# A two-layer hybrid trunk on one core: where the first mean stands, the order of attention's maxima, one late remainder, and how means are read

## The chip, the core and the metric

The kernel runs on one core of a Trainium2 chip. A core has TensorE (matmuls; in the profile PE, and PEld for its weight loads), VectorE (DVE), ScalarE (ACT), GpSimd (POOL) and SyncE (SP), which run side by side and wait for each other by semaphores, and 16 DMA engines that move data between the chip's main memory and the on-chip memory. TensorE writes its results to eight banks of 512 float32 columns by 128 rows; DVE and ACT read them from there. The metric is the time of one execution in device microseconds (us), as the median of several runs.

## The reference

Two layers, on 512 tokens of width 1024, all float32. The reference, cut to what matters:

```python
for l in range(DEPTH):                                             # 2 layers
    x = x + 0.5 * swiglu(rms_norm(x, ffn1_norm[l]), ffn1_w_in[l], ffn1_w_out[l])   # 1024 -> 2 x 2816 -> 1024
    h = rms_norm(x, mix_norm[l]) @ w_mix_in[l]                     # one projection for three mixers
    (c_x, c_b, c_c, h_q, h_f, h_i, h_g, f_q, f_k, f_v, f_f) = jnp.split(h, split_at, axis=-1)
    y = jnp.concatenate([
        short_conv_mixer(c_x, c_b, c_c, conv_w[l]),                # gated causal convolution, 3 taps, 256 channels
        hgrn2_mixer(h_q, h_f, h_i, h_g, ...),                      # 4 heads, linear recurrence, output norm per head
        fox_mixer(f_q, f_k, f_v, f_f, ...),                        # 8 heads, causal softmax attention with decay
    ], axis=-1)
    x = x + y @ w_mix_out[l]
    x = x + 0.5 * swiglu(rms_norm(x, ffn2_norm[l]), ffn2_w_in[l], ffn2_w_out[l])
```

`rms_norm` divides by the root of a mean of squares, `swiglu` is `(silu(gate) * up) @ w_out`. The attention subtracts each row's maximum before the exponential, as a softmax does.

## The kernel before

**Numbers.** Every large product is made of three matmuls (`mm3`, lines 494, 500 and 501): an operand is split into a high part, rounded by ACT (a cast, L475 or L1017), and a low part, the remainder, which DVE subtracts (L481 or L1019); high times high, high times low and low times high are added up in one bank. Activations are held with features on the rows and tokens on the columns. The moving operand of these matmuls is read `woven`: token t of the first half, token t of the second half, token t+1 of the first, and so on; the bank then holds the two halves alternating, and who reads it takes it apart again (`unwoven`).

**Feed-forward.** The hidden width has 22 tiles of 128. The first few (`covered`: 6 in the first feed-forward, 4 in the others) are made from the raw `x` in units of two tiles, eight steps along the depth in pairs, while the norm of `x` is still being made; `clear` divides the result by the norm afterwards. What else is done in that time stands in the table `ENTRY` by a due number: number n is the n-th pair of steps, and `deal(n)` is called ahead of each pair. It was also called at one quarter and at three quarters of a pair, for the due numbers of the means that end in .25 or .75. At a mean's due number `squares` has TensorE sum the squares of all features (`sum_norm`, L701 and L702, a matrix of 1/1024 times high and low part of the squares); at the due number of "norm" `take_norm` makes the inverse root out of it with a logarithm, two exponentials or squares on ACT and a Newton step on DVE. In the first feed-forward the mean has 4.25 and the norm 5; the second unit of two tiles starts at 4. There DVE first copies the mean out of the bank (L714).

The remaining tiles are worked in three chunks by a scheme that multiplies 2x2 blocks with seven products P1 to P7; `plan` lays the steps into the hidden layer ("I") and out of it ("O") in one sequence. Weights are cast three steps ahead (`LEAD`). The order of the work of ACT, DVE, SP and POOL in this part is written out (`follow`), as is TensorE's. In the last feed-forward a step out of the hidden layer adds its results into `xT` from the banks (L1090) in its second half (g = 1). A pair of hidden tiles of the last chunk leaves a split still to be made, a cast (L1228) and a subtraction (L1229); it is kept in `late` and made in the step after.

**Mix.** The mixers share TensorE: the generator `dense` (projections of attention), the convolution's projections and the output projection run beside `fox_attend`; the tuple `BESIDE` says how many pieces of them go between two steps of attention. Each head has two parts: p = 0 has the first two blocks of 128 queries in one bank, p = 1 the other two in a bank each. A part is: a mask into the bank and four matmuls (L1917); a maximum per block on DVE (L1933); an exponential on ACT with the row sums (L382, called at `scores`); the division; transposes (L1953), split into high and low (L1968, L1969); the products with the values (L1978). The output of a head is summed from two halves of the bank by DVE (L1996, two instructions), after ACT has copied one half (L1992). Here only TensorE's order is written out; that of DVE and ACT is chosen by the framework's planner from the order of the program, priorities and its own estimates of times. `add_manual_dep` with NOSYNC fixes an order of two instructions on an engine without a semaphore. Banks are guarded as a whole: an instruction of one engine on a bank waits for that of another engine ahead of it in the program.

The convolution's result is multiplied by its gate in `conv_out` (L1518), cast (L1520) and split (L1521), for its first tile and then its second (i = 1).

The HGRN mixer takes a mean over each head's 64 features with two matmuls (L1751, L1752) and the same `rsqrt`.

Of the kernel before, what the change touches and what calls it, by code (L numbers as in the profile page):

```python
# [14 lines left out]
ALU = mybir.AluOpType  # L15
# [235 lines left out]
class Trunk:  # L251
# [257 lines left out]
    def stream_steps(  # L509
# [17 lines left out]
        while k < nk:  # L527
# [60 lines left out]
            for n, ((acc, cols, toks, *more), j) in enumerate(order):  # L588
# [4 lines left out]
                for part in (1, 3) if deal is not None else ():  # L593
                    if n == part * len(order) // 4:
                        deal(k, part / 4)
# [76 lines left out]
    def rsqrt(self, out, v, r, t):  # L672

        nc = self.nc
        return [
            ("a", self.act(t, r, AF.Square)),
            ("v", nc.vector.scalar_tensor_tensor(
                out=t, in0=v, scalar=EPS, in1=t, op0=ALU.add, op1=ALU.mult
            )),
            ("v", nc.vector.tensor_scalar(t, t, scalar1=-0.5, scalar2=1.5, op0=ALU.mult, op1=ALU.add)),  # L680
            ("v", nc.vector.tensor_mul(out, r, t)),
        ]
# [14 lines left out]
    def sum_norm(self, bank, pool):  # L697
        if self.sqparts is None:
            self.part_norm(pool)
        (hi, lo), self.sqparts = self.sqparts, None  # L700
        self.nc.tensor.matmul(bank, self.ones_mean, hi, start=True, stop=False)  # L701
        return self.nc.tensor.matmul(bank, self.ones_mean, lo, start=False, stop=True)  # L702

    def take_norm(self, bank, pool, copied=False):

        mean = bank
        r = pool.tile([P, T], F32, tag=self.tt, name=self.n("nr"), bufs=self.tb)
        t = pool.tile([P, T], F32, tag=self.tt, name=self.n("nt"), bufs=self.tb)
        self.table(LNEXP)
        i = [("a", self.act(r, bank, AF.Ln, bias=self.epsc)), ("a", self.act(r, r, AF.Exp, scale=-0.5))]  # L710
        self.inv = self.res.tile([P, T], F32, tag="inv", name=self.n("inv"))
        if copied:
            mean = self.sqacc
            i.append(("v", self.nc.vector.tensor_copy(mean, bank)))  # L714
        return i + self.rsqrt(self.inv, mean, r, t)
# [228 lines left out]
    def halved(self, fp, w_in, w_out, covered, deal):  # L944
# [194 lines left out]
        for n, (kind, w, p) in enumerate(seq):  # L1139
# [87 lines left out]
            for hh, hl, y in late:  # L1227
                A(nc.scalar.copy(hh, y))  # L1228
                V(nc.vector.tensor_sub(hl, y, hh))  # L1229
            late = inner  # L1230
# [283 lines left out]
    def conv_out(self, pool, i, pb):  # L1514
# [3 lines left out]
        nc.vector.tensor_mul(halves(u), unwoven(pb), halves(y))  # L1518
# [5 lines left out]
    def hgrn(self, l, pr, hp, z, q, v, sg, og, S, kb, b, both):  # L1524
# [93 lines left out]
        halves = lambda lev: lambda a, i: a.rearrange(  # L1618
# [3 lines left out]
        def operands(lev):  # L1622
            w, half = 2**lev // 2, halves(lev)
# [20 lines left out]
        def score(lev, e, sb, at):  # L1644
# [9 lines left out]
            for i in range(4):  # L1654
                for hh, par in ((0, 0), (1, 1), (0, 1), (1, 0)):
# [4 lines left out]
                        out.rearrange("p (n w) -> p n w", w=2**lev // 2), keys, halves(lev)(keys, 1),  # L1660
# [3 lines left out]
        def place(lev, sb, at):  # L1664

            w, half = 2**lev // 2, halves(lev)
# [84 lines left out]
        nc.tensor.matmul(mb, self.ones_blk, sqh, start=True, stop=False)  # L1751
        nc.tensor.matmul(mb, self.ones_blk, sql, start=False, stop=True)  # L1752
        r, t = tmp(), tmp()
        self.act(r, mb, AF.Ln, bias=self.epsc)
        self.act(r, r, AF.Exp, scale=-0.5)
        self.rsqrt(r, mb, r, t)
# [138 lines left out]
    def fox_attend(self, pool, half, g):  # L1895
# [11 lines left out]
        def scores(h, p):  # L1907
# [22 lines left out]
            to = [pb[:, :P], pb[:, P:]] if p == 0 else [pb[:, : 3 * P], pb[:, 3 * P :]]  # L1930
            for u in range(2):
                o = slice(u, u + 1)
                nc.vector.tensor_reduce(nm[:, o], at[u], axis=AX.X, op=ALU.max, negate=True)  # L1933
                self.act(
                    turned_out(to[u]), inner(at[u]), AF.Exp,
                    bias=nm[:, o], accum_out=rs[:, o],
                )
# [33 lines left out]
        def values(h, p):  # L1971
# [22 lines left out]
            def add(to):  # L1994
                for n, b in ((0, slice(0, 4, 3)), (2, slice(1, 3))):
                    nc.vector.tensor_add(  # L1996
                        turned_out(to)[:, n : n + 2], inner(self.ob[:64, :])[:, b],
                        turned_out(ft[r, :])[:, b],
                    )

# [120 lines left out]
def trunk_kernel(  # L2121
# [5 lines left out]
    for l in range(DEPTH):  # L2127
        k.ffn(
            ffn1_w_in[l], ffn1_w_out[l], mix_norm[l], 4 if l else 6, 2 if l else 4.25,
# [39 lines left out]
```

## Time and profile before

| | |
|---|---|
| Median of 3 runs | 1742.44 us (1741.82 to 1742.48) |
| The profiled execution's own time | 1741.56 us |
| Its span, first to last instruction | 1739.8 us |
| TensorE: matmuls, weight loads | busy 1733.8 us (100%), 1627.5 us (94%) |
| DVE, ACT, POOL | busy 1413.9 us (81%), 1011.1 us (58%), 175.9 us (10%) |
| Granted TensorE clock | 1.000 of full speed |
| DMA | 262.29 MB, mean 151 GB/s |

A row of the timeline reads: start in us from the span's start, duration, engine, line of the program, operation, written tile <- read tiles, sizes, how many instructions are merged in the row, and in brackets the idle time of the engine just before, with what ended it. A row of the waits reads: engine, tile and line that waited <- engine, tile and line it waited for: us in total, times, longest. A row of the groups ends in busy us, mean ns of one instruction, and idle us before them. Matmuls are pipelined: the durations of neighbours overlap, so what a matmul costs is the distance of its start from the next one's.

### The profile page before, as it was taken

What the parts mean: (1) busy time and instruction counts of PE and PEld (TensorE: products, weight loads), DVE (VectorE), ACT (ScalarE), POOL (GpSimd) and SP (SyncE); (2) the same over time, 40 slices, a digit from 0 to 9 for tenths busy, and PEclk for the clock granted to TensorE, in tenths of its full rate; (3) what the DMA queues carried; (4) which work ended last, traced back from release to release, by engine and by line L of the source; (5) the groups of instructions that cost most, each with busy time, mean ns of one, the idle gap of its engine ahead of it and who ended that gap; (6) DMA issues with size and microseconds to landing.
All of it is one profiled execution on the core that took longest, in us unless ns stands there. A gap on an engine that the chain in (4) does not pass through costs nothing.

```text
span 1739.8 us, 32583 instructions
## 1 busy us (share of the span) xinstructions
PE 1733.8 (100%) x13215; PEld 1627.5 (94%) x13215; DVE 1413.9 (81%) x1926; ACT 1011.1 (58%) x1407; POOL 175.9 (10%) x174
## 2 busy tenths in 40 slices
PE   9999999999999999999999999999999999999999
PEld 7999999888888999999989999998888889999998
DVE  7988788778888898888689887876878779888884
ACT  5565565465766565566446556555657765655651
POOL 0011120100000112012001111201000000120210
PEclk9999999999999999999999999999999999999999
DMA  7768784243542966868267787923435437677672
GB/s 218 193 142 195 186 174 107 74 127 93 141 128 89 241 155 153 207 163 170 85 196 165 177 184 175 194 81 75 115 102 145 119 119 209 158 164 211 147 158 97
DMA packets 249766, 262.29 MB, mean 151 GB/s; under 512 B 25816, under 2 KB 221152, under 8 KB 249616
## 3 DMA queue, kind: packets, MB, share of 16 engines
q1 hardware_dynamic: 197344, 192.02, 37.0%
q0 software_dynamic: 52256, 68.19, 24.2%
q8 instruction: 104, 1.70, 0.4%
q14 instruction: 46, 0.38, 0.1%
q10 hardware_dynamic: 16, 0.00, 0.0%
HBM read 226.15 MB, written 2.17 MB: 131 GB/s over the span
## 4 chain that ended last, share of the span: by engine, by line
PE 96%; DVE 2%; ACT 1%; issue 0%; DMA 0%; SPq 0%; ACTq 0%
PE mm L494 10%; PE mm L501 10%; PE mm L500 10%; PE mm L580 9%; PE pt L500 7%; PE pt L494 7%; PE pt L501 7%; PE sc L500 6%; PE sc L494 6%; PE sc L501 6%; PE po L500 3%; PE po L494 3%; PE po L501 3%; PE po L580 2%; PE sc L1917 1%; PE po L1978 1%
## 5 line engine op out<-in xcount | busy, mean ns | idle before, releaser
L1019 DVE TENSOR_TENSOR hl<-w,hl 128x1024 fp32r<-128x1024 f32 x279 | 340.6, 1222 | 99.2 <-ACT hl L1017 97.9
L1017 ACT CAST hl<-w 128x1024 fp32r<-128x1024 f32 x279 | 292.6, 1049 | 204.3 <-PE mm L501 51.4
L481 DVE TENSOR_TENSOR hl<-st,hl 128x1024 fp32r<-128x1024 f32 (+3 forms) x152 | 159.8, 1054 | 93.5 <-ACT hl L475 92.8
L475 ACT CAST hl<-st 128x1024 fp32r<-128x1024 f32 (+3 forms) x151 | 137.3, 912 | 149.4 <-PE po L501 43.5
L501 PE MATMUL mm<-xc,hl 128*128 128x256 f32 x696 | 191.7, 275 | 0.0
L500 PE MATMUL mm<-xc,hl 128*128 128x256 f32 x696 | 191.7, 275 | 0.0
L494 PE MATMUL mm<-xc,hl 128*128 128x256 f32 x698 | 191.7, 275 | 0.0
L494 PE MATMUL pt<-xc,hl 128*128 128x256 f32 x546 | 150.2, 276 | 0.0
L500 PE MATMUL pt<-xc,hl 128*128 128x256 f32 x544 | 149.8, 275 | 0.0
L501 PE MATMUL pt<-xc,hl 128*128 128x256 f32 x544 | 149.7, 275 | 0.0
L494 PEld LDWEIGHTS mm<-xc,hl 128*128 128x128 f32 x698 | 134.0, 192 | 0.1
L501 PEld LDWEIGHTS mm<-xc,hl 128*128 128x128 f32 x696 | 133.7, 192 | 0.4 <-DVE hl L1019 0.4
L500 PEld LDWEIGHTS mm<-xc,hl 128*128 128x128 f32 x696 | 133.7, 192 | 0.0
L494 PE MATMUL sc<-xc,hl 128*128 128x256 f32 (+1 forms) x466 | 128.0, 275 | 0.0
L501 PE MATMUL sc<-xc,hl 128*128 128x256 f32 x464 | 127.8, 275 | 0.0
L500 PE MATMUL sc<-xc,hl 128*128 128x256 f32 x464 | 127.8, 275 | 0.0
L580 PE MATMUL mm<-hl,x 128*128 128x512 f32 x432 | 107.3, 384 | 0.0
L494 PEld LDWEIGHTS pt<-xc,hl 128*128 128x128 f32 x546 | 104.7, 192 | 0.3
L500 PEld LDWEIGHTS pt<-xc,hl 128*128 128x128 f32 x544 | 104.5, 192 | 0.3
L501 PEld LDWEIGHTS pt<-xc,hl 128*128 128x128 f32 x544 | 104.5, 192 | 0.0
L494 PE MATMUL mm<-x,hl 128*128 128x512 f32 x272 | 103.8, 381 | 0.0
L501 PE MATMUL mm<-x,hl 128*128 128x512 f32 x272 | 103.1, 380 | 0.2 <-DVE hl L481 0.2
(542 smaller groups left out, 5314.7 us busy)
## 6 DMA issues: line engine op xcount, KB each, us to landing
w<-in_ffn_w_in_dram SPq DMA_DIRECT2D x124, 512.0 KB
w<-in_ffn_w_out_dram POOLq DMA_DIRECT2D x50, 512.0 KB, 9.6
w<-in_ffn_w_out_dram SPq DMA_DIRECT2D x49, 512.0 KB
st<-in_ffn_w_out_dram SPq DMA_DIRECT2D x39, 512.0 KB
st<-in_w_mix_in_dram SPq DMA_DIRECT2D x72, 256.0 KB
st<-in_ffn_w_in_dram SPq DMA_DIRECT2D x71, 256.0 KB
w<-in_ffn_w_in_dram POOLq DMA_DIRECT2D x29, 512.0 KB, 10.1
w<-S POOLq DMA_DIRECT2D x29, 512.0 KB, 5.1
```

The costliest lines, as they stand in the source:

```text
L475: a = nc.scalar.copy(hi, src[:, c : c + w])
L481: b = nc.vector.tensor_sub(lo, src[:, c : c + w], hi)
L494: i = nc.tensor.matmul(acc[:, c], ah, bh[:, c.start // 2 : c.stop // 2, :], start=first and c.start == 0, stop=False, skip_group_check=True,)
L500: nc.tensor.matmul(acc, ah, bl, start=False, stop=False, skip_group_check=True)
L501: i = nc.tensor.matmul(acc, al, bh, start=False, stop=last, skip_group_check=True)
L580: self.follow("p", self.nc.tensor.matmul(acc, *((w, woven(x)) if toks is None else (x[:, toks], woven(w))), start=k == 0 and id(acc) not i ...
L1017: A(nc.scalar.copy(hi, src))
L1019: return lambda: V(nc.vector.tensor_sub(lo, src, hi))
L1917: mm = lambda *a, **k: E(nc.tensor.matmul(*a, skip_group_check=True, **k))
L1978: E(nc.tensor.matmul(self.ob[:, o * P : (o + len(at)) * P], half[2][:, j, h].rearrange("p a d -> p (a d)"), turned_in(part[:, at[0] : at[- ...
```

## The change

Five edits.

1. The mean of the first feed-forward has due number 4 instead of 4.25, so it is called ahead of the second unit's first pair of steps; the call of `deal` at one quarter of each pair is taken out.
2. The sums of squares are read `woven`, in the feed-forwards' norms and in the HGRN norm, and the mean's bank is read `unwoven` by the logarithm, the Newton step and the copy.
3. In attention's first part (p = 0) both maxima are issued ahead of both exponentials. The output sums of a head (L1996) may not be placed on DVE ahead of the maximum that was issued last.
4. Neither may the multiplication of the convolution's second tile (L1518 with i = 1).
5. In the last feed-forward, where the next step is the second half of a step out of the hidden layer, the pending split stays pending for that step too.

The function `halves` inside the HGRN mixer is called `sides` in the new text, so that the outer `halves` can be used; nothing else of it changes.

```diff
@@ stream_steps
-                for part in (1, 3) if deal is not None else ():
-                    if n == part * len(order) // 4:
-                        deal(k, part / 4)
+                if deal is not None and n == 3 * len(order) // 4:
+                    deal(k, 0.75)
@@ rsqrt
+        back = halves(t) if len(v.shape) != len(t.shape) else t
...
-                out=t, in0=v, scalar=EPS, in1=t, op0=ALU.add, op1=ALU.mult
+                out=back, in0=v, scalar=EPS, in1=back, op0=ALU.add, op1=ALU.mult
@@ sum_norm
-        self.nc.tensor.matmul(bank, self.ones_mean, hi, start=True, stop=False)
-        return self.nc.tensor.matmul(bank, self.ones_mean, lo, start=False, stop=True)
+        self.nc.tensor.matmul(bank, self.ones_mean, woven(hi), start=True, stop=False)
+        return self.nc.tensor.matmul(bank, self.ones_mean, woven(lo), start=False, stop=True)
@@ take_norm
-        mean = bank
+        mean = unwoven(bank)
...
-        i = [("a", self.act(r, bank, AF.Ln, bias=self.epsc)), ("a", self.act(r, r, AF.Exp, scale=-0.5))]
+        i = [
+            ("a", self.act(halves(r), unwoven(bank), AF.Ln, bias=self.epsc)),
+            ("a", self.act(r, r, AF.Exp, scale=-0.5)),
+        ]
...
-            i.append(("v", self.nc.vector.tensor_copy(mean, bank)))
+            i.append(("v", self.nc.vector.tensor_copy(halves(mean), unwoven(bank))))
@@ halved
-            for hh, hl, y in late:
-                A(nc.scalar.copy(hh, y))
-                V(nc.vector.tensor_sub(hl, y, hh))
-            late = inner
+            if last and n + 1 < len(seq) and seq[n + 1][0] == "O" and seq[n + 1][1][1]:
+
+                late = late + inner
+            else:
+                for hh, hl, y in late:
+                    A(nc.scalar.copy(hh, y))
+                    V(nc.vector.tensor_sub(hl, y, hh))
+                late = inner
@@ conv_out
-        nc.vector.tensor_mul(halves(u), unwoven(pb), halves(y))
+        m = nc.vector.tensor_mul(halves(u), unwoven(pb), halves(y))
+        if i:
+            self.tc.add_manual_dep(m.ins, self.maxima, NOSYNC, reason="given order")
@@ hgrn
-        nc.tensor.matmul(mb, self.ones_blk, sqh, start=True, stop=False)
-        nc.tensor.matmul(mb, self.ones_blk, sql, start=False, stop=True)
+        nc.tensor.matmul(mb, self.ones_blk, woven(sqh), start=True, stop=False)
+        nc.tensor.matmul(mb, self.ones_blk, woven(sql), start=False, stop=True)
...
-        self.act(r, mb, AF.Ln, bias=self.epsc)
+        self.act(halves(r), unwoven(mb), AF.Ln, bias=self.epsc)
...
-        self.rsqrt(r, mb, r, t)
+        self.rsqrt(r, unwoven(mb), r, t)
@@ fox_attend, scores
+            def maximum(u):
+                m = nc.vector.tensor_reduce(
+                    nm[:, u : u + 1], at[u], axis=AX.X, op=ALU.max, negate=True
+                )
+                self.maxima = m.ins.name
+
+            if p == 0:
+                maximum(0)
+                maximum(1)
             for u in range(2):
                 o = slice(u, u + 1)
-                nc.vector.tensor_reduce(nm[:, o], at[u], axis=AX.X, op=ALU.max, negate=True)
+                if p:
+                    maximum(u)
@@ fox_attend, values, add
-                    nc.vector.tensor_add(
+                    a = nc.vector.tensor_add(
                         turned_out(to)[:, n : n + 2], inner(self.ob[:64, :])[:, b],
                         turned_out(ft[r, :])[:, b],
                     )
+                    self.tc.add_manual_dep(a.ins, self.maxima, NOSYNC, reason="given order")
@@ trunk_kernel
-            ffn1_w_in[l], ffn1_w_out[l], mix_norm[l], 4 if l else 6, 2 if l else 4.25,
+            ffn1_w_in[l], ffn1_w_out[l], mix_norm[l], 4 if l else 6, 2 if l else 4,
```

More of the change, by code (lines that the diff above doesn't have):

```diff
@@ L1617, in hgrn @@
         A8 = A.rearrange("p h i t -> p (h i) t")
-        halves = lambda lev: lambda a, i: a.rearrange(
+        sides = lambda lev: lambda a, i: a.rearrange(
             "p (n two w) -> p n two w", two=2, w=2**lev // 2
@@ L1622, in operands @@
         def operands(lev):
-            w, half = 2**lev // 2, halves(lev)
+            w, half = 2**lev // 2, sides(lev)
             e = tmp()
@@ L1659, in score @@
                     nc.tensor.matmul(
-                        out.rearrange("p (n w) -> p n w", w=2**lev // 2), keys, halves(lev)(keys, 1),
+                        out.rearrange("p (n w) -> p n w", w=2**lev // 2), keys, sides(lev)(keys, 1),
                         start=True, stop=True,
@@ L1664, in place @@
         def place(lev, sb, at):
-            w, half = 2**lev // 2, halves(lev)
+            w, half = 2**lev // 2, sides(lev)
             if lev < 2:
```

## The prediction

> **What bounds the kernel now.** I read the page's busy times and its chain of waits first, then the waits of TensorE, then the timeline around each of them.
>
> ```profile
> PE 1733.8 (100%) x13215; PEld 1627.5 (94%) x13215; DVE 1413.9 (81%) x1926; ACT 1011.1 (58%) x1407; POOL 175.9 (10%) x174
> PE 96%; DVE 2%; ACT 1%; issue 0%; DMA 0%; SPq 0%; ACTq 0%
> ...
> PE mm L494 <- DVE xT L1090: 0.6, 1, 0.6
> PE sc L1917 <- ACT P L382: 0.4, 2, 0.2
> ```
>
> TensorE is busy for all but 6 of the span's 1739.8 us, its waits in these rows come to 0.6 and 0.4, and the chain that ended last is 96% TensorE. No transfer and no other engine sets the end. So the change can be worth only two things: matmuls that start closer together, and stops of TensorE that go or come. A stop costs more than its idle time, because matmuls overlap: I take it from one start to the next, less the usual step between starts.
>
> **The change part by part.** *Means read in turn.* Twenty matmuls sum squares: two for each of the trunk's six norms (L701, L702) and two for each of four pairs of HGRN heads (L1751, L1752). Their moving operand was read straight; now it alternates between the token halves, as every product's does.
>
> ```profile
> L500 PE MATMUL po<-x,hl 128*128 128x512 f32 x48 | 18.2, 379 | 0.0
> L701 PE MATMUL pt<-sqh,ones_mean 128*128 128x512 f32 x3 | 1.2, 399 | 0.0
> L1751 PE MATMUL sc<-t,ones_blk 128*128 128x512 f32 x4 | 1.6, 396 | 0.0
> ```
>
> A product of the same size lasts 379 ns, a mean 396 to 399 ns. In the next fence six products lie between 29.34 and 30.64 (0.217 each), and two means between 30.64 and 31.10 (0.23 each). So a mean gains 0.013 by the starts or 0.020 by the durations; twenty gain 0.26 to 0.40, I take 0.33. ACT and DVE now read the mean's bank in two halves. DVE does so in L1518 below at 0.69 us for 512 columns, as long as L714 straight; ACT's exponentials below read turned banks of 128, 256 and 384 columns in 0.37, 0.47 and 0.58, which carries on to 0.69 at 512, the straight logarithm's own. So that is nothing.
>
> [...]
>
> *First mean opens the second unit.*
>
> ```profile
> 27.89 0.69 DVE L694 TENSOR_TENSOR sql<-sqa,sqh 128x512 fp32r<-128x512 f32 x1
> ...
> 29.34 0.38 PE L494 MATMUL mm<-x,hl 128*128 128x512 f32 x1
> ...
> 30.64 0.40 PE L701 MATMUL po<-sqh,ones_mean 128*128 128x512 f32 x1
> ...
> 31.10 0.38 PE L494 MATMUL mm<-x,hl 128*128 128x512 f32 x1
> ...
> 31.30 0.69 ACT L382 ACTIVATE nr<-po,epsc 128x512 f32<-128x512 f32 x1 [3.67 <-PE po L702]
> ...
> 32.02 0.69 DVE L714 COPY sqa<-po 128x512 f32<-128x512 f32 x1 [1.32 <-ACT nr L382]
> ...
> 33.22 1.03 ACT L475 CAST hl<-st 128x1024 fp32r<-128x1024 f32 x1
> ...
> 35.14 1.22 DVE L481 TENSOR_TENSOR hl<-st,hl 128x1024 fp32r<-128x1024 f32 x1
> ...
> 35.85 0.38 PE L494 MATMUL mm<-x,hl 128*128 128x512 f32 x1
> 36.42 0.70 PE L501 MATMUL mm<-x,hl 128*128 128x512 f32 x2 [0.19 <-DVE hl L481]
> ```
>
> The mean stood six products into the second unit; it moves to its head, 1.30 us earlier. Its last operand (L694) is done at 28.58, 0.76 before 29.34, so TensorE need not wait. Everything from 31.30 to L481 stands in ACT's and DVE's written order behind the mean without a pause of its own, so L481 ends near 35.06 instead of 36.36, before the 36.07 (35.85 + 0.22) at which TensorE wants it. That removes 0.35 (36.42 − 36.07) and the slow restart behind it: the two matmuls of the last row start 0.32 apart (0.70 − 0.38), 0.10 over the step. Gain 0.45; lower bound 0, if the planner puts products ahead of the mean (this unit's are not chained). The removed call at one quarter of each unit had no other work: all other due numbers are whole, or at three quarters. L481 also frees its staging buffer, so the load behind it on SP starts earlier too, not later. Late next would be the following low part, 24 products (5.2 us) on; no bracket stands there now.
>
> *Maxima ahead of exponentials, output sums behind.* Eight heads, two layers, sixteen first parts; TensorE stops at one of them in each layer.
>
> ```profile
> 470.57 0.28 DVE L1933 TENSOR_REDUCE nm<-sc 128x1 f32<-128x128 f32 x1
> 470.93 0.37 ACT L382 ACTIVATE P<-sc,nm 128x128 f32<-128x128 f32 x1
> 470.94 0.74 DVE L1996 TENSOR_TENSOR fo<-po,t 64x256 f32<-64x256 f32 x2
> ...
> 471.61 0.41 DVE L1933 TENSOR_REDUCE nm<-sc 128x1 f32<-128x256 f32 x1
> ...
> 472.05 0.47 ACT L382 ACTIVATE P<-sc,nm 128x256 f32<-128x256 f32 x1 [0.66 <-DVE nm L1933]
> ...
> 472.23 0.22 PE L1917 MATMUL sc<-maskb,identb 128*128 128x128 bf16 x1
> ...
> 472.65 0.17 DVE L1938 RECIPROCAL rs<-rs 128x2 f32<-128x2 f32 x1 [0.63 <-ACT P L382]
> 472.67 0.22 PE L1917 MATMUL sc<-maskb,identb 128*128 128x128 bf16 x1 [0.21 <-ACT P L382]
> ```
>
> TensorE's second mask (472.67) needs the bank that the second exponential empties, near 472.61 (reciprocal behind it at 472.65). Two masks start 0.04 apart where nothing holds them (an estimate, from the 0.03 between mask and score at 467.83 below), so the stop is 0.40. Between the two maxima stand both output sums (0.74), longer than the first exponential, which frees ACT at 471.39 (472.05 − 0.66). New order: maxima 470.57 to 471.26, hop 0.08, first exponential 0.46 to 471.80, second 0.57 to 472.37: 0.25 earlier. The first exponential now waits for the second maximum, since both read one bank: L714 above likewise waited 1.32 for the logarithm on its bank. Behind it in ACT's queue stand the second exponential, which comes earlier all the same, and the cast of the next weights. Were both readers free to overlap, the whole 0.40 would go; were the maxima late for another reason, nothing. I take 0.25, two layers 0.50 (0 to 0.80). The sums move into the 0.63 that DVE idles before L1938; without that cover they cost DVE 0.74, TensorE nothing until the same output bank opens again, a head later.
>
> [...]
>
> *Convolution behind the maxima.* L1518 of the second convolution tile now follows the maxima of the fifth head's second part.
>
> ```profile
> 467.83 0.27 PE L1917 MATMUL sc<-maskb,identb 128*128 128x256 bf16 x1
> 467.86 0.30 PE L1917 MATMUL sc<-A 128*128 128x128 f32 x1
> ...
> 497.36 0.69 DVE L1518 TENSOR_TENSOR cu<-mm,cy 128x512 f32<-128x512 f32 x1
> ...
> 499.89 1.15 DVE L1933 TENSOR_REDUCE nm<-sc 128x1 f32<-128x384 f32 x2
> ...
> 500.54 0.58 ACT L382 ACTIVATE P<-sc,nm 128x384 f32<-128x384 f32 x1 [1.70 <-DVE nm L1933]
> ...
> 500.71 0.60 PE L1881 MATMUL pt<-ident,qk 128*128 128x128 f32 x4
> ...
> 501.26 0.27 PE L1917 MATMUL sc<-maskb,identb 128*128 128x256 bf16 x1
> 501.47 0.29 PE L1917 MATMUL sc<-S,S 128*128 128x128 f32 x1
> ...
> 504.40 0.38 PE L580 MATMUL mm<-cyh,hl 128*128 128x512 f32 x1
> ```
>
> The mask at 501.26 follows four transposes 0.11 apart (due 501.15), the score 0.21 behind it where 0.03 is usual (467.83 to 467.86): a stop of 0.11 + 0.18 = 0.29. It waits for the exponential of 500.54, which waits for maxima queued on DVE. L1518 out of the way moves them up by 0.6; the stop goes. L1518, its cast and its remainder land some 3.5 us later, near 502, still ahead of the first use of the convolution at 504.40. Both layers 0.58; lower bound 0, if other work takes the place.
>
> *Last remainder later.* Following the written sequence, a remainder is pending only once where the new branch applies: that of the second of the last chunk's three pairs of tiles (L1228 on ACT, L1229 on DVE).
>
> ```profile
> 1673.65 1.22 DVE L1229 TENSOR_TENSOR hh<-y,hh 128x1024 fp32r<-128x1024 f32 x1
> ...
> 1674.76 0.28 PE L501 MATMUL sc<-xc,hl 128*128 128x256 f32 x1
> 1674.78 1.28 DVE L1090 SCALAR_TENSOR_TENSOR xT<-mm,xT 128x512 f32<-128x512 f32 x2
> ...
> 1675.61 0.45 PE L494 MATMUL mm<-hl,m 128*128 128x512 f32 x1 [0.58 <-DVE xT L1090]
> 1675.90 0.38 PE L500 MATMUL mm<-hl,m 128*128 128x512 f32 x1
> 1675.98 1.22 DVE L1019 TENSOR_TENSOR hl<-S,hl 128x1024 fp32r<-128x1024 f32 x1
> ```
>
> TensorE is due at 1674.87 and waits for the first L1090 to empty its bank. With L1229 behind, the reads start at 1673.65 and the first ends at 1674.3. Gain 0.74 (1675.61 − 1674.87) plus a restart of 0.07 (1675.90 − 1675.61 − 0.22) = 0.81. The order is written out, so I see no lower bound but a new stop: L1228 (a cast) and L1229 now precede the weights of a step not due until two steps (5.3 us) after 1674.87; those are delayed by about 0.2.
>
> **Sum.** 0.33 + 0.45 + 0.50 + 0.58 + 0.81 = 2.67; all at their upper ends 3.04, all at their lower 1.07. The profiled execution took 1741.56, so 1738.9 in its terms; the median of the runs is 0.88 above it, so the forecast is 1739.8, 0.15% under 1742.44. About 0.2% (3.5 us) is what can be told from no change.
>
> **The rivals.** *Attention's stops stay* (1740.9): in the mix only TensorE's order is written out; the planner orders DVE from its own estimates and may put casts of transposed weights or weight parts where L1518 and the sums stood. The fixed orders of the opening and the last feed-forward are untouched by that. Gain 1.59. For it: those pieces already stand ahead of the maxima at 499.89. Against: the edges take away just the two pieces that lie there.
>
> *The mean does not move* (1740.2): the planner believes L694 later than the unit's head. Gain 2.22.
>
> *More goes than named* (1738.4): all upper ends, 3.04, and two or three of the other short stops, each like the 0.29 or 0.45 above, vanish with the altered order. For it: such stops exist. Against: nothing in the change names them.
>
> *Slower* (1747): the first exponential now stands behind the second maximum in ACT's queue in all sixteen places. If ACT has no slack there, each gives back up to 0.41 + 0.04 to the casts behind it and so to TensorE: 16 × 0.45 = 7.2, against the 2.2 that the other parts bring. It decides where the pair of exponentials ends later than now. Against: a hop fewer in the chain lets the pair end sooner, and ACT idles 0.66 there.
>
> *Alternating reads at half speed* (1744): then a mean's step doubles, 20 × 0.22 = 4.3 against 2.34 for the rest. The 0.217 of the products is against it. [...]
>
> **How the numbers follow.** Forecast 0.46; attention's stops stay 0.20; the mean does not move 0.07; more goes 0.17; slower 0.08; half speed 0.02. The forecast's own range is 1739.2 to 1740.6. Only "more goes" and the lowest tail of the forecast (0.05) pass 0.2%: faster 0.22. Slower by over 0.2% is the one case, 0.08; same 0.70. To hold 8 in 10 I leave out half of "more goes" below and the slower case above: 1737.8 to 1742.4.
>
> **What would show it.** Means with 379 ns; the first mean about 1.3 us earlier and L501 without the bracket of L481; the second mask less than 0.2 behind the first near 472; no gap before the score near 501; L1090 ahead of the remainder near 1673 and no stop there. I am wrong if TensorE has new brackets in the mix, or if the span falls by more than 3.5.

## The result

The changed kernel takes 1740.07 us (median of 22 runs, 1738.48 to 1742.94), the kernel before beside it 1743.05 us (22 runs, 1741.82 to 1746.89). The ratio is 0.9982, with a 95% interval from 0.9976 to 0.9988: 2.98 us faster, 0.17%. On another occasion it was 1739.75 against 1742.99 us: 0.9979 (0.9970 to 0.9988), 3.24 us. The forecast was 1739.8 us, that is 2.67 us off the time before.

The page of the changed kernel, its span, its busy times and the engines of its chain:

```profile
span 1738.2 us, 32601 instructions
...
PE 1733.3 (100%) x13215; PEld 1628.2 (94%) x13215; DVE 1414.1 (81%) x1926; ACT 1009.9 (58%) x1407; POOL 175.9 (10%) x174
...
PE 96%; DVE 2%; DMA 1%; issue 0%; ACT 0%; SPq 0%; DVEq 0%; ACTq 0%
```

The work of every engine is what it was; TensorE still sets the end. The waits of TensorE in the changed kernel (engine, tile and line <- what it waited for: us in total, times, longest):

```profile
PE po L2112 <- PEq L2175: 0.8, 1, 0.8
PE mm L494 <- ACT u L1195: 0.2, 1, 0.2
PE sc L500 <- DVE m L941: 0.2, 1, 0.2
```

Gone are the rows of before in which TensorE waited for `xT` (0.6), for attention's exponentials (0.4), for L481 (0.2) and, in the opening, for `x` (0.3). Two rows are new, a wait for ACT's L1195 and one for DVE's L941; they are taken up below. The five places, one by one, in the timeline of the changed kernel. First the opening's second unit:

```profile
29.68 0.38 PE L501 MATMUL pt<-x,hl 128*128 128x512 f32 x1
...
29.90 0.38 PE L701 MATMUL po<-sqh,ones_mean 128*128 128x512 f32 x1
...
30.53 0.69 ACT L382 ACTIVATE nr<-po,epsc 128x512 f32<-128x512 f32 x1 [2.34 <-PE po L702]
...
31.25 0.69 DVE L717 COPY sqa<-po 128x512 f32<-128x512 f32 x1
...
34.37 1.22 DVE L481 TENSOR_TENSOR hl<-st,hl 128x1024 fp32r<-128x1024 f32 x1
...
35.73 0.38 PE L500 MATMUL mm<-x,hl 128*128 128x512 f32 x1
...
35.94 0.38 PE L501 MATMUL mm<-x,hl 128*128 128x512 f32 x1
```

The mean follows the last product of the first unit at the usual step (29.68 to 29.90), the remainder L481 starts at 34.37 instead of 35.14 (0.77 earlier, though this execution reached the unit 0.56 later: 29.68 for the last product ahead of it, 29.12 in before), and L501 behind it starts 0.21 after the product ahead, with no bracket. The logarithm and the copy of the mean, which now take the bank apart, last 0.69, as before. The rows of the groups show the means themselves:

```profile
L1760 PE MATMUL sc<-t,ones_blk 128*128 128x512 f32 x4 | 1.5, 380 | 0.0
...
L701 PE MATMUL pt<-sqh,ones_mean 128*128 128x512 f32 x3 | 1.1, 379 | 0.0
```

379 to 380 ns instead of 396 to 399. Attention's first part that held TensorE near 472:

```profile
471.19 0.61 DVE L1942 TENSOR_REDUCE nm<-sc 128x1 f32<-128x128 f32 x2
...
471.72 0.73 DVE L2016 TENSOR_TENSOR fo<-po,t 64x256 f32<-64x256 f32 x2
...
471.83 0.37 ACT L382 ACTIVATE P<-sc,nm 128x128 f32<-128x128 f32 x1 [0.20 <-DVE nm L1942]
...
472.19 0.46 ACT L382 ACTIVATE P<-sc,nm 128x256 f32<-128x256 f32 x1
...
473.33 0.28 PE L1926 MATMUL sc<-maskb,identb 128*128 128x128 bf16 x2
...
473.42 0.41 PE L1926 MATMUL sc<-A 128*128 128x384 f32 x1
```

The two maxima are one row now, the output sums stand behind them, and the two masks have become one row of 0.28 (they are 0.44 apart in before, at 472.23 and 472.67), with the score at 473.42. One mask lasts 0.22, so the two now start 0.06 apart, and the stop that went is 0.38, in each layer. The second part, where L1518 (L1525 in the new text) was moved:

```profile
499.58 1.15 DVE L1942 TENSOR_REDUCE nm<-sc 128x1 f32<-128x384 f32 x2
...
500.22 0.58 ACT L382 ACTIVATE P<-sc,nm 128x384 f32<-128x384 f32 x1 [1.75 <-DVE nm L1942]
...
500.64 0.68 DVE L1525 TENSOR_TENSOR cu<-mm,cy 128x512 f32<-128x512 f32 x1
...
501.30 0.60 PE L1890 MATMUL pt<-ident,qk 128*128 128x128 f32 x4
...
501.74 0.27 PE L1926 MATMUL sc<-maskb,identb 128*128 128x256 bf16 x1
501.77 0.30 PE L1926 MATMUL sc<-S,S 128*128 128x128 f32 x1
```

The mask follows four transposes 0.11 apart exactly (501.30 + 0.44), and the score the mask by 0.03. A smaller stop just ahead of it has gone too, which the change does not name. In before three transposes waited for a subtraction on DVE, L1969, which stands behind L1518 in DVE's queue as the maxima do:

```profile
499.57 0.31 PEld L1953 LDWEIGHTS pt<-ident,P 128*128 128x128 f32 x3 [0.30 <-DVE PL L1969]
```

By the starts of the matmuls that cost 0.12 in each layer. It goes in every run in which the stop near 501 goes, and stays in every run in which that one stays. And the last feed-forward, where the remainder is now L1154:

```profile
1672.88 1.28 DVE L1093 SCALAR_TENSOR_TENSOR xT<-mm,xT 128x512 f32<-128x512 f32 x2
...
1674.10 0.38 PE L494 MATMUL mm<-hl,m 128*128 128x512 f32 x1
...
1674.32 0.38 PE L500 MATMUL mm<-hl,m 128*128 128x512 f32 x1
...
1675.30 1.22 DVE L1154 TENSOR_TENSOR hh<-y,hh 128x1024 fp32r<-128x1024 f32 x1
```

The additions into `xT` come first, the matmul starts with no bracket, 0.22 ahead of the next one, and the remainder follows two instructions later.

All five places are clean. Yet the span of this one execution is only 1.6 us shorter than that of before (1738.2 against 1739.8), where the medians differ by 2.98. The new wait for L1195 is one reason. The timeline at 82 to 86, changed kernel:

```profile
83.12 1.05 ACT L1020 CAST hl<-w 128x1024 fp32r<-128x1024 f32 x1 [2.29 <-DMA w<-S]
...
85.67 0.38 PE L494 MATMUL mm<-xc,hl 128*128 128x256 f32 x1 [0.23 <-ACT u L1195]
```

and the same cast in the kernel before:

```profile
82.26 1.05 ACT L1017 CAST hl<-w 128x1024 fp32r<-128x1024 f32 x1 [1.61 <-DMA w<-S]
```

A cast waits for a transfer that adds into the weight; the cast started 0.86 later in the trace of after, ACT's queue moved back with it, and TensorE stopped for 0.67 by the starts of its matmuls, up to 89 us. The stop at this place is 0 in before's trace and 0 to 1.4 us in the traces of the experiments, in kernels that do not differ ahead of it as well.

The wait for L941, near 102.6, is a stop of before that is 0.12 longer here, and about 0.1 longer in kernels that do not differ ahead of it. The opening took 0.56 more: there the first two matmuls of L548 last 0.80 and 0.58, against 0.48 and 0.38 in before, and until 6.5 us TensorE's steps are about twice as long (two matmuls of 512 columns at 4.55 start 0.43 apart, in before at 4.50 they start 0.22 apart); the granted clock reads 1.00 there in both traces, so what slowed the opening is not shown. And near 383.4 a stop of 0.33 stands in this trace alone. Together that is 1.7. The terms of the change, counted below, come to 3.1, and 3.1 less 1.7 is 1.4 of the 1.6 that this pair of spans shows. The second trace of the same kernel, in the timed set, has other values at these places (0.35 in the opening, 0.38 at 85 us, no stop at 383), so they belong to the execution, not to the change.

### The profile page after: what moved, and what is told of

Same layout as the page of the kernel before. It is cut to its first block, busy times and chain, and to the rows that moved or that the text cites. A ratio compares the mean times of both kernels' runs of the same rounds, so it can differ in the third digit from the quotient of the medians.

```text
span 1738.2 us, 32601 instructions
## 1 busy us (share of the span) xinstructions
PE 1733.3 (100%) x13215; PEld 1628.2 (94%) x13215; DVE 1414.1 (81%) x1926; ACT 1009.9 (58%) x1407; POOL 175.9 (10%) x174
## 4 chain that ended last, share of the span: by engine, by line
PE 96%; DVE 2%; DMA 1%; issue 0%; ACT 0%; SPq 0%; DVEq 0%; ACTq 0%
PE mm L494 11%; PE mm L501 11%; PE mm L500 11%; PE mm L580 9%; PE pt L500 6%; PE pt L494 6%; PE pt L501 6%; PE sc L500 6%; PE sc L494 6%; PE sc L501 6%; PE po L500 3%; PE po L501 3%; PE po L494 3%; PE po L580 2%; PE sc L1926 1%; PE po L1998 1%
## 5 line engine op out<-in xcount | busy, mean ns | idle before, releaser
L481 DVE TENSOR_TENSOR hl<-st,hl 128x1024 fp32r<-128x1024 f32 (+3 forms) x152 | 159.8, 1054 | 95.7 <-ACT hl L475 94.5
L501 PE MATMUL mm<-xc,hl 128*128 128x256 f32 x696 | 191.7, 275 | 0.0
L501 PE MATMUL pt<-xc,hl 128*128 128x256 f32 x544 | 149.7, 275 | 0.0
L501 PEld LDWEIGHTS mm<-xc,hl 128*128 128x128 f32 x696 | 133.7, 192 | 0.3 <-DVE hl L1022 0.3
L501 PE MATMUL sc<-xc,hl 128*128 128x256 f32 x464 | 127.8, 275 | 0.0
L501 PEld LDWEIGHTS pt<-xc,hl 128*128 128x128 f32 x544 | 104.5, 192 | 0.0
L501 PE MATMUL mm<-x,hl 128*128 128x512 f32 x272 | 103.1, 379 | 0.0
```

The source lines that it names most:

```text
L481: b = nc.vector.tensor_sub(lo, src[:, c : c + w], hi)
L501: i = nc.tensor.matmul(acc, al, bh, start=False, stop=last, skip_group_check=True)
```

## The experiments

The first eight kernels have one time each, which is good for 2 us or so: the kernel before took 1743.88 beside the first four and 1742.40 beside the next four. There the verdict rests on the timeline, on the stops of TensorE from one start to the next. Line numbers shift by a few between kernels.

### The first mean alone, and a mean later still

```diff
@@ stream_steps
-                for part in (1, 3) if deal is not None else ():
-                    if n == part * len(order) // 4:
-                        deal(k, part / 4)
+                if deal is not None and n == 3 * len(order) // 4:
+                    deal(k, 0.75)
@@ trunk_kernel
-            ffn1_w_in[l], ffn1_w_out[l], mix_norm[l], 4 if l else 6, 2 if l else 4.25,
+            ffn1_w_in[l], ffn1_w_out[l], mix_norm[l], 4 if l else 6, 2 if l else 4,
```

> The kernel before with the first mean at 4 alone. Theory (the norm's chain in the written orders of ACT and DVE sets the stop): the mean starts near 29.3 instead of 30.64, the subtraction L481 ends near 35.1 instead of 36.36, and the stop of 0.45 at 36.42 is gone. Rival (the stop is a late transfer, or the planner puts products ahead of the mean): the mean stays near 30.6, or L481 still ends near 36.4 and the stop stays. If the changed kernel's new stop at 85.67 (0.67 us, a cast that waits for an accumulating transfer) comes from the earlier mean, it is here too; if it comes from transfers that vary from run to run, it is here only by chance.

It took 1742.03 us. The stop at 36.42 is gone: from 29 to 50 us TensorE's steps are 0.45 too long in before and 0.00 here. The stops near 473, 502 and 1676 are there as before (0.38 for the first). So this edit is worth its 0.45, and it moves the mean as it says.

The other way round, with the mean half a unit later than in before:

```diff
@@ trunk_kernel
-            ffn1_w_in[l], ffn1_w_out[l], mix_norm[l], 4 if l else 6, 2 if l else 4.25,
+            ffn1_w_in[l], ffn1_w_out[l], mix_norm[l], 4 if l else 6, 2 if l else 4.75,
```

> The kernel before with the first mean at 4.75 instead of 4.25, twelve products (2.6 us) later. Theory (each us of the mean's place is a us of the chain): the stop of 0.45 grows by 2.6 to about 3.0, and the time by 2.6. Rival (the stop comes from a transfer or another queue): the stop changes by much less than 2.6.

It took 1744.94 us. The stop grew, but by less than the delay, and it moved to another place. The timeline:

```profile
35.55 0.48 PE L494 MATMUL po<-x,hl 128*128 128x512 f32 x1 [1.50 <-DVE sqa L714]
```

Now the bank of the mean itself is wanted back before DVE has copied it; then smaller stops follow for the low parts (0.28 at 39.19). In all TensorE's steps are 2.3 to 2.4 too long there, against 0.45: 1.9 more, where I expected 2.6. TensorE's order may show why it is less: at 37.61 to 38.69 it takes the products with the high parts of three rows first and leaves all their L501, which need the low parts, for 39.19. So another order seems to cover part of the delay; no run here fixed the order to test that.

### The turned reading alone

```diff
@@ sum_norm
-        self.nc.tensor.matmul(bank, self.ones_mean, hi, start=True, stop=False)
-        return self.nc.tensor.matmul(bank, self.ones_mean, lo, start=False, stop=True)
+        self.nc.tensor.matmul(bank, self.ones_mean, woven(hi), start=True, stop=False)
+        return self.nc.tensor.matmul(bank, self.ones_mean, woven(lo), start=False, stop=True)
@@ hgrn
-        nc.tensor.matmul(mb, self.ones_blk, sqh, start=True, stop=False)
-        nc.tensor.matmul(mb, self.ones_blk, sql, start=False, stop=True)
+        nc.tensor.matmul(mb, self.ones_blk, woven(sqh), start=True, stop=False)
+        nc.tensor.matmul(mb, self.ones_blk, woven(sql), start=False, stop=True)
...
```

> The kernel before with the means read in turn alone. Theory: the starts of the twenty means lie 0.216 apart as those of products do, instead of 0.23, 0.33 us in all; the named stops stay as before. [...]

It took 1742.76 us. All twenty means start 216 ns ahead of the next matmul and last 379; before, the mean of the twenty steps is 234 ns (4.67 us in all, 4.32 now). That is 0.35 us, and the named stops all stay (0.45 at 36.7, 0.38 at 473.6, 0.74 at 1676.5 by its main step). One more thing changed: at 451 a stop of TensorE became 0.07 longer, in both layers. In the timeline of before it is the step from 449.58 to 449.95,

```profile
449.58 0.38 PE L501 MATMUL mm<-x,hl 128*128 128x512 f32 x1
...
449.95 0.45 PE L494 MATMUL mm<-x,hl 128*128 128x512 f32 x1
```

0.37; in the changed kernel it is 0.44, from 450.66 to 451.10:

```profile
450.66 0.38 PE L501 MATMUL mm<-x,hl 128*128 128x512 f32 x1
...
451.10 0.45 PE L494 MATMUL mm<-x,hl 128*128 128x512 f32 x1
```

It stands in every kernel that reads the means in turn and in none of the others. It lies just behind the HGRN norm, so the planner's order there is likely, but no run took it apart.

### How a matmul's time depends on the order in which it reads

The changed kernel with fifteen more matmuls ahead of each of the six norms' means, three for each of five orders. Their sums are overwritten by the mean that follows, so they only cost time.

```diff
@@ sum_norm
+        runs = lambda w: lambda x: x.rearrange("p (h t w) -> p t h w", h=2, w=w)
+        quarters = lambda x: x.rearrange("p (h t) -> p t h", h=4)
+        for read in (woven, lambda x: x, runs(2), runs(4), quarters):
+            for _ in range(3):
+                self.follow("p", self.nc.tensor.matmul(bank, self.ones_mean, read(hi), start=True, stop=True))
```

> The changed kernel with fifteen matmuls more ahead of each of the six means, three for each of five orders in which the same 512 columns are read: halves in turn, straight, halves in turn in runs of two, in runs of four, quarters in turn. Their sums are overwritten. Theory (a straight read is what costs, and any turn between distant places is free): straight about 0.23 from start to start, the four others 0.216. Rival (what counts is how many neighbouring words are read together): the step grows or falls step by step from turns through runs of two and four to straight. [...]

It took 1762.52 us. The view of the line over the whole run gives the shortest, the median and the longest of 45 durations in ns, the timeline the first three, which read the halves in turn (two steps and one duration of 0.38 make 0.81):

```profile
L705 PE MATMUL po<-sqh,ones_mean x45: 379/418/518, 29.6 to 1452.3; 128*128 128x512 f32 x45
```

```profile
29.60 0.81 PE L705 MATMUL po<-sqh,ones_mean 128*128 128x512 f32 x3
```

From the starts in the trace, for 512 columns of the same data:

| order of the reads | start to start, ns | duration, ns |
|---|---|---|
| halves in turn (one from each, `woven`) | 216 | 379 |
| straight | 230 to 246, about 235 | 397 |
| runs of four from each half | 246 to 265, about 255 | 418 |
| quarters in turn | 272 to 283, about 278 | 443 |
| runs of two from each half | 319 to 348, about 328 | 501 |

Neither expectation holds. The time does not follow the length of the runs, and a jump at every element need not cost anything: the halves in turn jump at every element and have the step of a product, while the quarters in turn do so too and take 62 ns more. The gain of the edit is real, but it is a property of this one order.

### The pair of maxima alone

```diff
@@ fox_attend, scores
+            if p == 0:
+                maximum(0)
+                maximum(1)
             for u in range(2):
                 o = slice(u, u + 1)
-                nc.vector.tensor_reduce(nm[:, o], at[u], axis=AX.X, op=ALU.max, negate=True)
+                if p:
+                    maximum(u)
```

> The kernel before with the two maxima of attention's first part ahead of both exponentials, and no edge for the output sums. Theory (the length of the chain maximum, exponential, maximum, exponential sets the stop of 0.40 at the second mask near 472.67 and 1334.30): the sums slip behind the pair by themselves or stand ahead of it as a whole; the pair is 0.25 to 0.5 shorter and the stop at most 0.15. Rival (the sums between the maxima are what costs): they still stand ahead of the second exponential's release, and the stop stays near 0.40.

It took 1742.45 us, of which 1.69 are a lowered clock at 393 us (below, under what the runs showed). Both of attention's stops are gone, in both layers, though neither the output sums nor L1518 have an edge. The timeline of DVE and of TensorE:

```profile
494.23 0.61 DVE L1933 TENSOR_REDUCE nm<-sc 128x1 f32<-128x128 f32 x2
494.76 0.74 DVE L2007 TENSOR_TENSOR fo<-po,t 64x256 f32<-64x256 f32 x2
495.83 0.17 DVE L1949 RECIPROCAL rs<-rs 128x2 f32<-128x2 f32 x1 [0.33 <-ACT P L382]
...
498.48 0.68 DVE L1518 TENSOR_TENSOR cu<-mm,cy 128x512 f32<-128x512 f32 x1
...
501.01 1.15 DVE L1933 TENSOR_REDUCE nm<-sc 128x1 f32<-128x384 f32 x2
```

```profile
502.40 0.60 PE L1881 MATMUL pt<-ident,qk 128*128 128x128 f32 x4
...
502.84 0.27 PE L1917 MATMUL sc<-maskb,identb 128*128 128x256 bf16 x1
502.87 0.30 PE L1917 MATMUL sc<-S,S 128*128 128x128 f32 x1
```

The same head in the kernel before, DVE:

```profile
492.86 0.28 DVE L1933 TENSOR_REDUCE nm<-sc 128x1 f32<-128x128 f32 x1
...
494.72 0.17 DVE L1938 RECIPROCAL rs<-rs 128x2 f32<-128x2 f32 x1 [0.31 <-ACT P L382]
```

Two things follow. Once the two maxima stand together, the planner puts the sums behind them by itself. And the stop near 501 hangs on the same head's first part: from the reciprocal to the next maxima DVE has a chain of work that is 5.17 long in before (494.72 to 499.89) and 5.18 here (495.83 to 501.01), with L1518 still in it. It starts earlier, since the first part takes 1.60 from its first maximum to the reciprocal instead of 1.86, and since that maximum itself stands 0.32 earlier against TensorE's transposes (1.37 later than in before, where the transposes are 1.69 later); why it stands earlier, no run shows. Together the second part's maxima come 0.57 earlier against TensorE, more than the 0.29 of the stop.

### The edge of the sums alone, the edge of the convolution alone

```diff
@@ fox_attend, values, add
-                    nc.vector.tensor_add(
+                    a = nc.vector.tensor_add(
...
+                    self.tc.add_manual_dep(a.ins, self.maxima, NOSYNC, reason="given order")
```

> The kernel before with the output sums behind the last maximum alone. Theory (the chain's hops count, the sums cost 0.2 of them): the second maximum starts near 471.43 instead of 471.61, and the stop at 472.67 falls from 0.40 to about 0.2. Rival (the sums are the whole cause): the stop is gone. The stop near 501 stays at 0.29 in both.

It took 1742.44 us. The timeline of attention's first part, with each maximum still in front of its own exponential:

```profile
472.38 0.42 DVE L1933 TENSOR_REDUCE nm<-sc 128x1 f32<-128x256 f32 x1 [0.58 <-ACT P L382]
...
472.84 0.47 ACT L382 ACTIVATE P<-sc,nm 128x256 f32<-128x256 f32 x1 [0.49 <-DVE nm L1933]
...
473.18 0.49 PE L1917 MATMUL sc<-maskb,identb 128*128 128x128 bf16 x2
```

The two masks are now 0.27 apart (0.49 for both less 0.22 for one), where 0.06 is usual: the stop is 0.2 by the starts, instead of 0.38. The sums are out of the way, yet the second maximum waits 0.58 for the first exponential on the same bank, and ACT then waits 0.49 for the maximum. This is the cost of the alternation itself, which of these edits only the pair removes. The stop near 502 stays.

```diff
@@ conv_out
-        nc.vector.tensor_mul(halves(u), unwoven(pb), halves(y))
+        m = nc.vector.tensor_mul(halves(u), unwoven(pb), halves(y))
+        if i:
+            self.tc.add_manual_dep(m.ins, self.maxima, NOSYNC, reason="given order")
```

> The kernel before with the convolution's second product behind the maxima alone. Theory: the maxima of the fifth head's second part start 0.6 earlier against TensorE, and the stop of 0.29 near 501 and 1363 is gone; the stops of 0.40 near 472 and 1334 stay. Rival (the planner puts other work in that place): the maxima stay where they were and so does the stop.

It took 1742.48 us. L1518 stands at 502.02, behind the maxima at 500.96; the stops near 501 and 1363 are gone and those at 474.19 and 1335.42 stay, 0.38 each. So this edge alone does what was said of it, and so does the pair: either is enough for the stop near 501.

### The last remainder alone

```diff
@@ halved
+            if last and n + 1 < len(seq) and seq[n + 1][0] == "O" and seq[n + 1][1][1]:
+                late = late + inner
+            else:
...
```

> The kernel before with the last remainder later alone. Theory (DVE's written order keeps the reads L1090 behind the remainder): L1090 starts near 1673.65 instead of 1674.78, and the stop of 0.81 at 1675.61 is gone, with no stop of more than 0.1 in the next ten us. Rival (the wait moves on to the next weights, whose cast now stands behind the remainder's cast): a stop of 0.2 or more within two steps (5.3 us) behind it.

It took 1742.35 us. The additions into `xT` start at 1675.26, the matmul that waits for them follows at the usual step, and from there to 1705 no step of TensorE is over 0.1 too long; the two at 1706 (0.19 and 0.10) are those of before. The stop that goes is not the same in each run: 0.74 by its main step in the run with only the means turned, 0.96 in the run with only the convolution's edge.

### Two halves, the whole, and the whole without the two edges

Timed side by side, with 33 runs of the kernel before (1742.99 us). First the changed kernel without its attention edits:

```diff
@@ conv_out, add (against the changed kernel)
-            self.tc.add_manual_dep(m.ins, self.maxima, NOSYNC, reason="given order")
...
-                    self.tc.add_manual_dep(a.ins, self.maxima, NOSYNC, reason="given order")
@@ fox_attend, scores
-            if p == 0:
-                maximum(0)
-                maximum(1)
...
-                if p:
-                    maximum(u)
+                maximum(u)
```

> Edits 1, 2 and 5 together, attention and convolution as before. Theory (the terms are separate and add up): 0.45 + 0.33 + 0.81 = 1.6 us faster than before. Rival (the gain comes mostly from the altered order in the mix): under 0.8 us.

1741.29 us, ratio 0.9992 (0.9983 to 1.0001): 1.70 us. Then the attention edits alone, the pair and both edges, on the kernel before:

```diff
@@ fox_attend, scores (against the kernel before)
+            if p == 0:
+                maximum(0)
+                maximum(1)
...
@@ conv_out, add
+            self.tc.add_manual_dep(m.ins, self.maxima, NOSYNC, reason="given order")
...
+                    self.tc.add_manual_dep(a.ins, self.maxima, NOSYNC, reason="given order")
```

> Edits 3 and 4 together, all else as before. Theory: both stops of attention go in both layers, 2 x 0.40 + 2 x 0.29 = 1.4 us faster than before (1.1 by the forecast's 0.25 for the first stop). Rival (attention's stops are given back in later waits): under 0.5 us.

1741.66 us, ratio 0.9992 (0.9983 to 1.0001): 1.33 us. Each interval just holds 1, so neither half is told from no change by itself; the stops in the traces say that both are real. Beside them the whole change, unaltered:

> The changed kernel itself, on the same chip as the others. Theory: the sum of the two halves, 2.7 (the forecast) to 3.0 us faster than before. Rival (the halves overlap or feed other waits): less than the larger half alone and more than 0.7 away from the sum.

1739.75 us, ratio 0.9979 (0.9970 to 0.9988): 3.24 us, and the two halves add up to 3.03. The difference is less than the intervals can tell, so nothing shows that the halves help or hinder each other. Last the whole without the edges on the sums and on the convolution:

```diff
@@ conv_out, add (against the changed kernel)
-            self.tc.add_manual_dep(m.ins, self.maxima, NOSYNC, reason="given order")
...
-                    self.tc.add_manual_dep(a.ins, self.maxima, NOSYNC, reason="given order")
```

> The changed kernel without the two orders for the output sums and the convolution; the maxima stand ahead of the exponentials in the program alone. Theory after the single look at that edit (the planner moves the rest by itself once the pair is short): as fast as the changed kernel, within 0.3 us, no stop near 472 or 501. Rival (each of the two orders is needed): the stops near 501 and 1363 are back and it is 0.6 us slower than the changed kernel.

1739.54 us, ratio 0.9982 (0.9973 to 0.9990), as fast as the whole: 0.21 us in the medians is less than the intervals can tell. In its trace neither of attention's stops is there. With the pair in place the two edges are not needed.

## Why the prediction was right, step by step

The sum of terms stood at 2.67 us, and 2.98 and 3.24 were measured. The time itself, 1740.07 for 1739.8, fits better than the gain by luck: the kernel before came out 0.6 us slower in the later runs than in the three known ahead. The sum is short because one term was too small and one stop was not named; a loss that was not seen hid part of that. Term by term, by the starts of TensorE's matmuls:

| term | forecast | measured |
|---|---|---|
| means in turn | 0.33 | 0.35 |
| the first mean at the unit's head | 0.45 | 0.45 |
| attention's first part, two layers | 0.50 | 0.76 |
| attention's second part, two layers | 0.58 | 0.59 |
| transposes ahead of the second part, two layers | not seen | 0.24 |
| last remainder later | 0.81 | 0.82 |
| longer stop behind the HGRN norm, two layers | not seen | -0.13 |
| sum | 2.67 | 3.08 |

- **The mean.** Right in each link: the sum of squares was ready, the chain behind it moved as one, and L481 came before TensorE wanted it. The late mean shows that this chain sets the stop, though the stop grew by less than the delay (1.9 for 2.6). The rival in which the mean does not move (0.07) is out.
- **The turned reading.** Right in size. That reading it back costs ACT and DVE nothing was right too: 0.69 before and after.
- **The pair of maxima.** The direction was right, the size was not: this is the term that was mis-sized, 0.25 per layer where 0.38 went. I had the second exponential start 1.23 after the first maximum (0.69 for two maxima, a hop of 0.08, 0.46 for the first exponential); in the rows of after it starts 1.00 after it (471.19 to 472.19), where before has 1.48 (470.57 to 472.05). So it comes 0.48 earlier, not 0.25. The durations that I added up overlap when one engine follows itself: both maxima take 0.61, the first exponential starts 0.64 after the first maximum, and the second 0.36 after the first. The old order lost, beside the sums' time, a change of engine in each direction: with the sums alone out of the way DVE still waited 0.58 and ACT then 0.49, and less than half of the stop went (0.38 to 0.2). Nearly the upper end of 0.40 was the result, but not for the reason given there: the first exponential did wait for the second maximum (it starts at 471.83, both maxima end at 471.80).
- **The edges.** Half right. The edge on the convolution does what I said of it, alone. What I said against the rival in which attention's stops stay, that the edges take away just the pieces that lie in the way, is not what decides: the pair does, and the planner follows. I had treated the two stops as separate, and had not seen the 0.12 in front of the second that went with it; the second one hangs on the first part of the same head by a chain of 5.2 us on DVE.
- **The last remainder.** Right, with no new stop behind it; the delayed split was not late for anybody.
- **The slower rival**, in which the first exponential behind the second maximum costs ACT's queue up to 0.45 in sixteen places, is out for the reason given against it: the pair ends sooner.
- **More going than named** is out by its time, 1738.4, but came true in small: the stop of 0.12 per layer at the transposes went with the altered order, though nothing in the change names it. Behind the opening no other stop of over 0.1 went. The rest of what went beyond the sum is the pair.
- **Half speed** for the alternating reads is out: 216 ns. The doubling was my estimate, and no run shows it: the slowest of the five orders has a step of 328 ns, 1.5 times the 216.
- **The signs of being wrong** did not come: no row of TensorE's waits lies in the mix (the stop near 383.4 is in one of the two traces alone), and the span fell by 1.6.
- **Not foreseen** were the 0.07 per layer behind the HGRN norm, and how much one execution can hide: the profiled one shows 1.6 of the 3 us, because of a transfer that landed late, an opening that was 0.56 slower and two smaller stops. A reader of that one span would have called the forecast too high.

## What to carry to other kernels

Where two engines take turns on one bank (maximum, exponential, maximum, exponential), try the readings of one engine together: here the second exponential came 0.48 earlier that way, and the planner then moved the rest by itself. Before adding an ordering edge for each piece that stands in the way, ask which stops hang on one another: here one edit cured both of attention's, and a third that nobody had named. And with changes of a tenth of a per cent, read the stops one by one in the timeline: a single span holds a microsecond or two of chance (1.7 here).

## What the runs showed of the hardware

**The order of reads.** The table above: for the same 512 columns the step goes from 216 to 328 ns with the order alone, and the straight read is not the fastest. The halves in turn, which jump at every element, are the fastest (216), the runs of two are the slowest (328). What orders the five cases, no run here shows.

**A clock that drops in the middle of the work.** In four traces (the pair alone, the two halves and the whole of the timed set) TensorE's granted clock is about half for one stretch of 3.4 us, behind the HGRN's 64 matmuls of two columns, and full before and after: 0.51 over that stretch in the pair alone and in the attention edits, 0.54 and 0.58 in the other two, whose windows begin a little behind the drop (0.98 and 0.97 in the 8.5 us ahead). The windows of the pair alone (stretch, its length, then busy time of PE, PEld, DVE, ACT and POOL with counts, then the granted clock, the DMA share and GB/s):

```profile
385.00:393.00 8.00, 8.00 (x95) 6.64 (x94) 7.66 (x16) 5.76 (x11) 0.00 (x0) 1.00 0.40 113
393.00:396.40 3.40, 3.40 (x10) 2.70 (x9) 3.40 (x9) 1.65 (x4) 0.00 (x0) 0.51 0.35 77
396.40:404.00 7.60, 7.60 (x37) 6.66 (x36) 7.60 (x16) 7.04 (x12) 0.00 (x0) 1.00 0.00 0
```

and the same stretch of the changed kernel's first trace:

```profile
393.00:396.40 3.40, 3.40 (x27) 3.01 (x25) 3.40 (x9) 2.67 (x6) 0.00 (x0) 1.00 0.32 77
```

Matmuls of 512 columns then start 0.426 apart instead of 0.216, and the stretch costs 1.69 us in each of the four traces. It comes in the first layer (three traces) or the second (one), and the same changed kernel has it in one trace and not in the other, so it belongs to the execution. TensorE was issuing without a stop ahead of it (busy 8.00 of 8.00 us from 385 to 393): the drop begins 0.3 to 0.6 us behind the last of the 64 matmuls of two columns, which take 1.8 us. Whether these bring it on, no run here tested; the other traces have the same 64 without a drop.

**A transfer's landing.** The stop at 85.7 us in the first feed-forward was anything from 0 to 1.4 us long, behind one transfer that adds into a weight. With the clock's 1.69 this may be most of the scatter between runs of one kernel: among the 22 runs of the changed kernel, the three with a mean granted clock of 0.999 took 1741.76 to 1741.95 us, against a median of 1740.07, and a stretch of 3.4 us at half clock lowers the mean by just that 0.001.
